# A GELU-gate kernel: 8-row tiles with two DMA queues, and 16-row blocks with one

## The chip, the core and the metric

The kernel runs on one core of a Trainium2 chip. The time is the device time of one execution in microseconds (us). Of the kernel before there are nine runs. Besides, one execution was recorded by the hardware profiler; all rows of "the profile" are from that one execution, with times counted from the first instruction of its span. In it DVE is VectorE, ACT is ScalarE, SP is SyncE, POOL is GpSimd; TensorE has no work here. "SPq" and "ACTq" are the instruction streams of SP and ACT as far as they issue DMAs. L81 is line 81 of the kernel.

## What is computed

```
x: float32 [32, 512, 2048]
x1, x2 = x[..., :1024], x[..., 1024:]
out = 0.5 * x1 * (1 + erf(x1 / sqrt(2))) * x2      # float32 [32, 512, 1024]
```

The input is 134.2 MB, the output 67.1 MB. Each value is read once, each result written once.

## The kernel before

The 32 x 512 = 16384 rows are cut into 16 tiles. A tile holds 8 rows (`R`) for each of the 128 partitions: partition p of a tile has 8 rows that follow one another in memory, so a load brings 64 KB of contiguous bytes to each partition (8.39 MB a tile), and a store takes 32 KB from each (4.19 MB).

There are two input buffers and two output buffers, used by turns (`k = i % 2`). For each tile, two steps of 5 and 3 rows: ACT computes gelu of the first half of each row into the output buffer (L81), then DVE multiplies the output buffer by the second half, in place (L89). The first and last tile are cut into three steps of 2, 2 and 4 rows.

The order of the work is written out by hand, with semaphores:

- Loads are all issued by SP (`load`, L47). The first tile's load is cut into two of 4 rows; it and tile 1's load are issued before anything else. In the loop, the load of tile i + 2 is issued when the multiplies of tile i are done (L108, L109), as it overwrites the same input buffer.
- Stores are issued by ACT (`store`, L54; called in L101 and L106) after the tile's multiplies, so that ACT's stream waits for DVE there. The store of tile 14 and the two half stores of tile 15 are issued by SP.
- Gelu of tile i waits on `ready[k]` (L79), which counts the load of tile i into input buffer k and the store that empties output buffer k: both must have landed.

Hence two queues carry DMAs at the same time, SP's with 64 KB for each partition and ACT's with 32 KB. Both run on the same 16 DMA engines. The kernel ends when SP has seen the last stores land (L118).

Of the kernel before, what the change touches and what calls it, by code (L numbers as in the profile page):

```python
# [1 line left out]

# [4 lines left out]

GELU = mybir.ActivationFunctionType.Gelu


@with_exitstack
def kernel(
    ctx: ExitStack,
    tc: tile.TileContext,
    x: bass.AP,
    out: bass.AP,
):
    nc = tc.nc
    P = nc.NUM_PARTITIONS

    x_flat = x.flatten_outer_dims()
    out_flat = out.flatten_outer_dims()
    n_rows, dim = x_flat.shape
    half = dim // 2

    R = 8
    x_t = x_flat.rearrange("(n p r) d -> n p r d", p=P, r=R)
    o_t = out_flat.rearrange("(n p r) d -> n p r d", p=P, r=R)
    n_tiles = x_t.shape[0]
    x_bufs = [nc.alloc_sbuf_tensor(f"x{k}_tile", [P, R, dim], x.dtype) for k in range(2)]  # L30
    o_bufs = [nc.alloc_sbuf_tensor(f"o{k}_tile", [P, R, half], out.dtype) for k in range(2)]

    first = [nc.alloc_semaphore(f"first{j}") for j in range(2)]
    ready = [nc.alloc_semaphore(f"ready{k}") for k in range(2)]
    gelu_done = nc.alloc_semaphore("gelu_done")
    mul_done = nc.alloc_semaphore("mul_done")
    tail_stored = nc.alloc_semaphore("tail_stored")
    n = {sem.name: 0 for sem in [*first, *ready, gelu_done, mul_done, tail_stored]}  # L40

    def counted(ins, sem, by):
        ins.then_inc(sem, by)
        n[sem.name] += by

    def load(i, rows, sem):
        ins = nc.sync.dma_start(out=x_bufs[i % 2][:, rows, :], in_=x_t[i][:, rows, :])  # L47
        counted(ins, sem, 16)
        return ins

    def store(queue, i, rows, sem):
        queue.wait_ge(mul_done, n[mul_done.name])
        counted(
            queue.dma_start(out=o_t[i][:, rows, :], in_=o_bufs[i % 2][:, rows, :]), sem, 16  # L54
        )

    for ins in (  # L60
        load(0, slice(0, 4), first[0]),
        load(0, slice(4, 8), first[1]),
        load(1, slice(0, 8), ready[1]),
    ):
        tc.no_tile_sem_insts.add(ins.ins.name)
    tc.close()
    tc.compile()  # L67

    for i in range(n_tiles):
        k = i % 2  # L70
        last = i == n_tiles - 1
        pieces = i == 0 or last
        steps = ((0, 2), (2, 4), (4, 8)) if pieces else ((0, 5), (5, 8))
        for lo, hi in steps:
            rows = slice(lo, hi)
            if i == 0 and lo % 4 == 0:
                nc.scalar.wait_ge(first[lo // 4], 16)
            elif lo == 0:
                nc.scalar.wait_ge(ready[k], n[ready[k].name])  # L79
            counted(  # L80
                nc.scalar.activation(  # L81
                    out=o_bufs[k][:, rows, :], in_=x_bufs[k][:, rows, :half], func=GELU
                ),
                gelu_done,
                1,
            )
            nc.vector.wait_ge(gelu_done, n[gelu_done.name])
            counted(
                nc.vector.tensor_mul(  # L89
                    out=o_bufs[k][:, rows, :],  # L90
                    in0=o_bufs[k][:, rows, :],
                    in1=x_bufs[k][:, rows, half:],
                ),
                mul_done,
                1,
            )
            if pieces and hi % 4 == 0:
                if last:
                    store(nc.sync, i, slice(hi - 4, hi), tail_stored)
                else:  # L100
                    store(nc.scalar, i, slice(hi - 4, hi), ready[k])  # L101
        if not pieces:
            if i == n_tiles - 2:
                store(nc.sync, i, slice(0, R), tail_stored)
            else:
                store(nc.scalar, i, slice(0, R), ready[k])  # L106
        if i + 2 < n_tiles:
            nc.sync.wait_ge(mul_done, n[mul_done.name])  # L108
            load(i + 2, slice(0, R), ready[k])  # L109


    nc.scalar.drain()  # L112
    for sem in (*first, *ready):
        nc.scalar.sem_clear(sem)
    nc.vector.drain()
    nc.vector.sem_clear(gelu_done)
    nc.sync.sem_clear(mul_done)
    nc.sync.wait_ge(tail_stored, n[tail_stored.name]).then_inc(  # L118
        tail_stored, -n[tail_stored.name]
    )  # L120


# [1 line left out]
_INS = ['x']  # L124
_OUTS = [((32, 512, 1024), 'float32')]


# [23 lines left out]
```

## Time and profile before

| What | Value |
|---|---|
| Median of nine runs | 469.21 us (469.13 to 469.47) |
| Profiled execution | 469.15 us |
| Its span, first to last instruction | 467.8 us |
| VectorE busy | 140.5 us, 34 multiplies |
| ScalarE busy | 115.5 us, 34 gelus and a table load |
| Gelu of 5 rows, of 3 rows | 4.47 us, 2.75 us |
| Multiply of 5 rows, of 3 rows | 5.49 us, 3.35 us |
| Read from HBM, written to it | 134.22 MB, 67.11 MB: 430 GB/s over the span |
| SP's DMA queue (q1) | 142.61 MB, 70.6% of the 16 engines' span |
| ACT's DMA queue (q10) | 58.72 MB, 29.1% |
| Store of a tile by ACT, issue to landing | 44.7 us (median of 13) |
| Load of a tile by SP, issue to landing | 44.3 us (median of 15) |
| ACT's gelu waited for a store to land | 301.7 us in 14 waits |
| ACT's gelu waited for a load | 35.6 us in 3 waits |

How to read it: a share of a queue is the time that its packets took, as a share of the time of 16 DMA engines over the span. "Issue to landing" runs from the instruction that starts a DMA until its last byte is reported. A wait is put down to what came last: gelu waits for a load and a store at once, and the profile names the later one.

### The profile page before, as it was taken

The page shows a single profiled execution, that of the slowest core. Times are in us where ns is not written, and L with a number is a line of the kernel's source. Part 1 is how long each engine was busy: PE and PEld are TensorE (multiplying, and loading weights), DVE is VectorE, ACT ScalarE, POOL GpSimd, SP SyncE. Part 2 cuts the span into 40 slices and gives each one's busy share as a digit, 9 for nine tenths or more (in the row PEclk, how much of TensorE's full clock was granted, in tenths as well). Part 3 has the DMA queues.
Part 4 walks back from the last instruction along what each step waited for, and adds up shares of the span by engine and source line. Part 5 has one row for each costly group of instructions (what it writes and reads, how often), then busy time and mean ns, then how long its engine had stood idle before and what let it go on. Part 6 is the DMA issues. An engine that isn't in the chain of part 4 may idle for free.

```text
span 467.8 us, 152 instructions
## 1 busy us (share of the span) xinstructions
DVE 140.5 (30%) x34; ACT 115.5 (25%) x35; POOL 0.2 (0%) x4
## 2 busy tenths in 40 slices
DVE  0330515207052060511606116060150702507043
ACT  1320606042060410604106050050500506014060
POOL 0000000000000000000000000000000000000000
DMA  8999999999999999999999999999999999999988
GB/s 359 448 448 448 415 389 496 403 403 448 448 448 403 434 417 493 403 403 448 482 415 403 445 406 493 403 403 448 488 409 403 448 420 476 403 420 431 493 381 382
DMA packets 5041, 201.34 MB, mean 430 GB/s; under 512 B 560, under 2 KB 560, under 8 KB 560
## 3 DMA queue, kind: packets, MB, share of 16 engines
q1 hardware_dynamic: 2880, 142.61, 70.6%
q10 hardware_dynamic: 2160, 58.72, 29.1%
q14 instruction: 1, 0.01, 0.0%
HBM read 134.22 MB, written 67.11 MB: 430 GB/s over the span
## 4 chain that ended last, share of the span: by engine, by line
DMA 76%; DVE 14%; ACT 8%; ACTq 0%; SPq 0%; issue 0%
DMA out_dram<-o_tile 66%; DVE o_tile L89 14%; DMA x_tile<-in_x_dram 10%; ACT o_tile L81 8%; ACTq L112 0%; SPq L47 0%
## 5 line engine op out<-in xcount | busy, mean ns | idle before, releaser
L89 DVE TENSOR_TENSOR o_tile<-o_tile,x_tile 128x5120 f32<-128x5120 f32 (+3 forms) x34 | 140.5, 4171 | 319.7 <-ACT o_tile L81 319.7
L81 ACT ACTIVATE o_tile<-x_tile 128x5120 f32<-128x5120 f32 (+3 forms) x34 | 114.3, 3407 | 337.4 <-DMA out_dram<-o_tile 301.7
L81 ACT ACT_TABLE_LOAD x1 | 1.3, 1283 | 2.8 <-PEq L67 2.8
L135 POOL MEMSET const-bfloat16-1.0<- 128x1 bf16 x1 | 0.1, 102 | 0.0
L135 POOL MEMSET const-uint8-127<- 128x1 uint8 x1 | 0.1, 102 | 0.0
L135 POOL MEMSET const-float32-1.0<- 128x1 f32 x1 | 0.1, 99 | 0.0
L135 POOL MEMSET const-float32-0.0<- 128x1 f32 x1 | 0.1, 98 | 0.2 <-issue 0.2
## 6 DMA issues: line engine op xcount, KB each, us to landing
out_dram<-o_tile ACTq DMA_DIRECT2D x13, 4096.0 KB, 44.7
x_tile<-in_x_dram SPq DMA_DIRECT2D x2, 4096.0 KB, 16.7
out_dram<-o_tile ACTq DMA_DIRECT2D x2, 2048.0 KB, 34.4
out_dram<-o_tile SPq DMA_DIRECT2D x1, 4096.0 KB, 25.2
out_dram<-o_tile SPq DMA_DIRECT2D x2, 2048.0 KB, 7.8
x_tile<-in_x_dram SPq DMA_DIRECT2D x15, 44.3
```

The lines of the kernel that those rows point to most:

```text
L81: nc.scalar.activation(out=o_bufs[k][:, rows, :], in_=x_bufs[k][:, rows, :half], func=GELU),
L89: nc.vector.tensor_mul(out=o_bufs[k][:, rows, :], in0=o_bufs[k][:, rows, :], in1=x_bufs[k][:, rows, half:],),
L135: nc = _bacc.Bacc("TRN2", target_bir_lowering=False, num_devices=1)
```

## The change

Two tiles become one block of 16 rows a partition. The block has two loads, A (its first 8 rows of each partition) and B (the other 8), each 64 KB a partition into its own input buffer, and one store of 64 KB a partition out of a single output buffer of 16 rows. All DMAs are issued by SP, in the order load A, store, load B; ACT issues none. The output buffers hold as many bytes as before.

- `load(b, h)`: half h of block b. The rows of neighbouring partitions now lie 128 KB apart in the input (64 KB before), and 64 KB apart in the output (32 KB before).
- Load A of block b + 1 is issued when A's multiplies of block b are done; the store of block b when B's are done, and load B of block b + 1 right after it.
- Gelu of half A waits on `ready[0]`: its load and the store of the block before. Gelu of half B waits on `ready[1]`: its load alone.
- The first block's loads are not cut (two whole loads are issued ahead instead of two halves and a whole one), and its steps are 5 and 3 rows. The last block's first half is stored by itself (32 KB a partition), its second half in steps of 2, 2 and 4 rows with two stores of 16 KB a partition.
- The multiplies and gelus are otherwise the same: 34 of each before and, with the first block's steps, 33 of each after. There are 26 DMAs instead of 35.

```diff
-    x_t = x_flat.rearrange("(n p r) d -> n p r d", p=P, r=R)
-    o_t = out_flat.rearrange("(n p r) d -> n p r d", p=P, r=R)
+    x_t = x_flat.rearrange("(n p h r) d -> n h p r d", p=P, h=2, r=R)
+    o_t = out_flat.rearrange("(n p r) d -> n p r d", p=P, r=2 * R)
...
-    o_bufs = [nc.alloc_sbuf_tensor(f"o{k}_tile", [P, R, half], out.dtype) for k in range(2)]
+    o_buf = nc.alloc_sbuf_tensor("o_tile", [P, 2 * R, half], out.dtype)
...
+    def load(b, h):
+        return counted(nc.sync.dma_start(out=x_bufs[h][:, :, :], in_=x_t[b, h]), ready[h], 16)
+
+    def store(b, rows, sem):
+        nc.sync.wait_ge(mul_done, n[mul_done.name])
+        counted(nc.sync.dma_start(out=o_t[b][:, rows, :], in_=o_buf[:, rows, :]), sem, 16)
...
-    for ins in (
-        load(0, slice(0, 4), first[0]),
-        load(0, slice(4, 8), first[1]),
-        load(1, slice(0, 8), ready[1]),
-    ):
-        tc.no_tile_sem_insts.add(ins.ins.name)
+    for h in range(2):
+        tc.no_tile_sem_insts.add(load(0, h).ins.name)
...
+    for b in range(n_blocks):
+        last = b == n_blocks - 1
+        for h in range(2):
+            nc.scalar.wait_ge(ready[h], n[ready[h].name])
+            for lo, hi in ((0, 2), (2, 4), (4, 8)) if last and h else ((0, 5), (5, 8)):
+                xr, orow = slice(lo, hi), slice(h * R + lo, h * R + hi)
...
+                if last and h and hi % 4 == 0:
+                    store(b, slice(R + hi - 4, R + hi), tail_stored)
+            if last and not h:
+                store(b, slice(0, R), tail_stored)
+            elif not last:
+                if h:
+                    store(b, slice(0, 2 * R), ready[0])
+                nc.sync.wait_ge(mul_done, n[mul_done.name])
+                load(b + 1, h)
```

More of the change, by code (lines that the diff above doesn't have):

```diff
@@ L26 @@
     R = 8
-    x_t = x_flat.rearrange("(n p r) d -> n p r d", p=P, r=R)
-    o_t = out_flat.rearrange("(n p r) d -> n p r d", p=P, r=R)
-    n_tiles = x_t.shape[0]
+    x_t = x_flat.rearrange("(n p h r) d -> n h p r d", p=P, h=2, r=R)
+    o_t = out_flat.rearrange("(n p r) d -> n p r d", p=P, r=2 * R)
+    n_blocks = x_t.shape[0]
     x_bufs = [nc.alloc_sbuf_tensor(f"x{k}_tile", [P, R, dim], x.dtype) for k in range(2)]
-    o_bufs = [nc.alloc_sbuf_tensor(f"o{k}_tile", [P, R, half], out.dtype) for k in range(2)]
-    first = [nc.alloc_semaphore(f"first{j}") for j in range(2)]
+    o_buf = nc.alloc_sbuf_tensor("o_tile", [P, 2 * R, half], out.dtype)
     ready = [nc.alloc_semaphore(f"ready{k}") for k in range(2)]
@@ L39 @@
     tail_stored = nc.alloc_semaphore("tail_stored")
-    n = {sem.name: 0 for sem in [*first, *ready, gelu_done, mul_done, tail_stored]}
+    n = {sem.name: 0 for sem in [*ready, gelu_done, mul_done, tail_stored]}
     def counted(ins, sem, by):
@@ L44, in counted @@
         n[sem.name] += by
-    def load(i, rows, sem):
-        ins = nc.sync.dma_start(out=x_bufs[i % 2][:, rows, :], in_=x_t[i][:, rows, :])
-        counted(ins, sem, 16)
-        return ins
[L51 to L55, printed above, removed]
-    for ins in (
-        load(0, slice(0, 4), first[0]),
-        load(0, slice(4, 8), first[1]),
-        load(1, slice(0, 8), ready[1]),
-    ):
-        tc.no_tile_sem_insts.add(ins.ins.name)
+        return ins
@@ L66 @@
+    def load(b, h):
[5 more added lines that the diff above has]
+        tc.no_tile_sem_insts.add(load(0, h).ins.name)
     tc.close()
     tc.compile()
[L69 to L109, printed above, removed]
@@ new lines @@
+    for b in range(n_blocks):
[4 more added lines that the diff above has]
+                xr, orow = slice(lo, hi), slice(h * R + lo, h * R + hi)
+                counted(
+                    nc.scalar.activation(
+                        out=o_buf[:, orow, :], in_=x_bufs[h][:, xr, :half], func=GELU
+                    ),
+                    gelu_done,
+                    1,
+                )
+                nc.vector.wait_ge(gelu_done, n[gelu_done.name])
+                counted(
+                    nc.vector.tensor_mul(
+                        out=o_buf[:, orow, :],
+                        in0=o_buf[:, orow, :],
+                        in1=x_bufs[h][:, xr, half:],
+                    ),
+                    mul_done,
+                    1,
+                )
+                if last and h and hi % 4 == 0:
[7 more added lines that the diff above has]
+                load(b + 1, h)
@@ L112 @@
     nc.scalar.drain()
-    for sem in (*first, *ready):
+    for sem in ready:
         nc.scalar.sem_clear(sem)
```

## The prediction, written before the changed kernel was run

> **What bounds the kernel now.** I read the page's busy lines first, then its slices, then the chain, the windows and the timeline.
>
> ```profile
> span 467.8 us, 152 instructions
> DVE 140.5 (30%) x34; ACT 115.5 (25%) x35; POOL 0.2 (0%) x4
> ...
> DMA  8999999999999999999999999999999999999988
> ...
> DMA 76%; DVE 14%; ACT 8%; ACTq 0%; SPq 0%; issue 0%
> ```
>
> No compute engine is busy for a third of the span; the DMA row is full except at its two ends. The chain names DVE and ACT for 22%, but that is only how one transfer is followed back through the buffer that it filled. Three stretches, asked for by window, decide between "the DMA engines are the limit" and "a loop of waits is the limit":
>
> ```profile
> 0.00:1.70 1.70, 0.00 (x0) 0.00 (x0) 0.20 (x4) 1.00 0.00 0
> 1.70:467.40 465.70, 140.49 (x34) 115.54 (x35) 0.00 (x0) 1.00 1.00 432
> 467.40:467.80 0.40, 0.00 (x0) 0.00 (x0) 0.00 (x0) 1.00 0.00 0
> ```
>
> The last two columns are the busy share of the 16 DMA engines and GB/s. Nothing moves for 1.7 us, then all engines are busy for 465.7 us, then 0.4 us pass until the last landing is seen. So the DMA engines' own time is the limit, not waits. Any kernel that moves these 201.3 MB at this rate can only gain at the ends or in the price of a packet.
>
> The steady period, from the timeline:
>
> ```profile
> 100.51 7.12 ACT L81 ACTIVATE o_tile<-x_tile 128x5120 f32<-128x5120 f32 x2 [21.88 <-DMA out_dram<-o_tile]
> 105.02 8.76 DVE L89 TENSOR_TENSOR o_tile<-o_tile,x_tile 128x5120 f32<-128x5120 f32 x2 [20.24 <-ACT o_tile L81]
> 113.81 0.36 ACTq L54 DMA_DIRECT2D out_dram<-o_tile  x1
> 129.51 7.12 ACT L81 ACTIVATE o_tile<-x_tile 128x5120 f32<-128x5120 f32 x2 [21.88 <-DMA out_dram<-o_tile]
> ```
>
> A tile (8.39 MB in, 4.19 MB out) takes 129.51 - 100.51 = 29.00 us, which is 434 GB/s, or 9.667 us for each 4.19 MB. From the first gelu of a tile to the end of its second multiply it is 113.80 - 100.51 = 13.3 us; call this the compute of a half block.
>
> The trace's packet records (one record for each piece that one DMA engine moves; here one partition's row of a DMA) give the price of a piece. From start to start on one engine: 64 KB 2.414 us, 32 KB 1.2095 us, 16 KB 0.607 us, and 0.0055 us more where one DMA ends and the next of the same queue begins. Eight pieces of 64 KB and eight of 32 KB make 28.99 us, which is the period: the engines run without gaps, and loads and stores cost the same per byte.
>
> **The change part by part.**
>
> *Same bytes, other pieces.* Before, for one DMA engine: loads 15 x 8 x 2.414 + 2 x 8 x 1.2095 = 309.03; stores 14 x 8 x 1.2095 + 4 x 8 x 0.607 = 154.89; together 463.92 us. After: 16 loads x 8 x 2.414 = 308.99; seven stores of 64 KB a partition 7 x 8 x 2.414 = 135.18; the half block 8 x 1.2095 = 9.68; two quarters 2 x 8 x 0.607 = 9.71; together 463.56. That is -0.36 us. DMAs go from 35 to 26: 9 x 0.0055 = -0.05. Sum **-0.4 us**. A 64 KB store piece is not in the trace; I price it as a 64 KB load piece, since at 32 KB both have a 1213 ns record. At two 32 KB pieces it would be 2.419, and this term -0.1.
>
> *The second queue goes.* Before, when the first store (ACT's queue) came beside the third load, the 64 KB records there were longer than 2418 ns, and again a little later: 0.39 us for a mean engine, all before 80 us. After, there is one queue and the first store comes at about 60 us behind work of its own queue. This can vanish (-0.39) or come back whole (0). I take half: **-0.2 us**.
>
> *One queue in order: does it run dry?* SP now issues everything: load A waits for A's multiplies, and behind it in SP's order stand the store and load B, which wait for B's multiplies. Follow one handover. When the store of block b lands, gelu of A(b+1) may start, since there is one output buffer. Its data landed 19.3 us earlier, as load A stands ahead of the store. It needs 13.3 us, then SP issues A(b+2). Meanwhile load B(b+1) runs for 2 x 9.667 = 19.3 us. The other handover is alike: B(b+1) lands, 13.3 us of compute, then the store and load B(b+2) are issued, while load A(b+2) runs for 19.3 us. A landing is seen 0.4 us after the last packet (467.4 to 467.8 above), and an issue needs 1.0 us to its first packet (0.73 to 1.7). So 13.3 + 0.4 + 1.0 = 14.7 us stand under a cover of 19.3 us: **slack 4.6 us**, cost nothing. If compute and latencies came to 19.3 + d, each of some 14 handovers would cost d.
>
> Does ACT or DVE slow down when the traffic beside it is all loads or all stores? The four 128x2048 multiplies ran two beside loads only (from 14.7 us) and two beside stores only (from 450.5 us); the pairs took 4.49 and 4.50 us. No.
>
> *The start.* Compute starts at about 22.5 us instead of 12.80, since the first load is whole. Loads A and B fill the queue until 1.7 + 0.6 (the first packets' excess) + 38.6 = 40.9 us; A's compute ends at 22.5 + 13.3 = 35.8, so the next issue again has 4 us of slack. Cost nothing; the old early store only filled a queue that was full.
>
> *The end.* The last loads land, then the half-block store (9.68 us, issued long before) covers the compute: the first quarter is ready 0.4 + 6.5 us after the last load (448.53 to 454.99 now), needed at 9.68; the second after 0.4 + 11.7 (to 460.22), needed at 14.5. No gap; the last DMA is 2 MB as before, so the end is unchanged. Before has this very sequence: load 15, store 14 and the last two stores, all on SP's queue:
>
> ```profile
> 432.80 27.76 SPq L54 DMA_DIRECT2D out_dram<-o_tile  x3
> 448.53 7.22 ACT L81 ACTIVATE o_tile<-x_tile 128x2048 f32<-128x2048 f32 x3 [21.89 <-DMA out_dram<-o_tile]
> ...
> 455.78 4.42 DVE L89 TENSOR_TENSOR o_tile<-o_tile,x_tile 128x4096 f32<-128x4096 f32 x1 [0.81 <-ACT o_tile L81]
> ```
>
> From 448.51 to 467.8 it stored 8.39 MB in 19.3 us, the steady rate. So pure stores on one queue, and load-then-store on one queue, are shown at full speed; so are pure loads (first two landings, 12.80 and 22.51: 9.71 us).
>
> *Store, then load, on one queue* happens seven times and is not in this trace. Nearest row: load to load, load to store and store to store, 0.0055 us each. Far row: the first packets of a cold engine, which were 0.6 us longer than the following ones. Below nothing there is nothing: no engine idles that a turn could fill. I take **0** (the queue has work behind it, as in the near rows); the far end is 7 x 0.6 = +4.2 us.
>
> *A rule against it.* The row pitch in HBM doubles: 128 KB between the partitions' rows of a load (64 KB before), 64 KB for a store (32 KB before). At the old pitches every steady packet took 2418 or 1213 ns. The trace shows no other pitch. The Trainium skill, "DMA: Bandwidth & Descriptors", section "Latency and other measured facts", says that copies between HBM tensors lose rate when the rows lie large powers of two apart: 207 GB/s at 512 KiB against 214 when padded, 164 at 2 MiB. As an estimate from that page, if its 512 KiB loss (3.3%) struck all loads, the time would be some 10 us more, about 478.7; its list starts above our pitch, so I count it as nothing.
>
> **Sum.** The profiled execution took 469.15 us (span 467.8 and 1.35 around it; the median of the runs is 469.21, 0.06 more). 469.15 - 0.4 - 0.2 = **468.55 us**.
>
> **Rivals.**
> 1. *Faster: the losses around the packets go too.* 465.7 us of traffic hold 463.9 + 0.2 us of pieces; some 1.5 us are the first packets' excess (0.6), the mixing (0.39) and the stagger of the 16 engines. A single orderly queue might lose less. Floor: 1.7 + 463.56 + 0.14 + 0.4 + 1.35 = 467.2. For it: the losses sit where queues start. Against: the 0.6 belongs to the cold start, which stays. With the mixing and most of the 0.6 gone: 467.8.
> 2. *Slower: the turn from store to load.* If the engine drained its store before it read again, every turn would cost up to 0.6 us: 468.55 + 4.2 = 472.8; at 0.35, 471.0. It decides from (470.15 - 468.55)/7 = 0.23 us a turn. Against: before, each engine goes from a store piece to a load piece eight times a tile, and the period equals the sum of pieces.
> 3. *The order does not hold or the queue does not take DMAs ahead*, so that each of 26 DMAs pays 1.0 + 0.4 us: 468.55 + 36 = 505. Against: store 14 was issued at 432.80 behind load 15 and ran after it without a gap.
>
> **Chances.** A measurement of this kernel can tell about 0.2% (0.94 us) from no change: faster means under 468.27, slower over 470.15. The forecast lies 0.3 us from the first bound, so the faster case takes a good share: forecast and what lies about it 0.60, rival 1 0.25, rival 2 0.12, rival 3 and the pitch 0.03. The range goes from the floor, 467.2, to the far end of the turns, 472.8; the forecast's own range, from the ends of its two terms, is 468.3 to 469.1.
>
> **What would show it.** Right: DMA share 1.00 from 1.7 us to 0.4 us before the end; blocks 58.0 us apart; gelu of A waiting for the store's landing, some 2 x 19.3 - 7.1 = 31.5 us, and gelu of B for load B's, 19.3 - 7.1 = 12.2 us; the SP queue's waits all for DVE. Wrong: a DMA share under 1 after each store (rival 2); records of 64 KB above 2418 ns through the steady part (pitch); handovers where an issue comes less than 1 us before the load in flight ends (slack); compute rows longer than 4.47 and 5.49 us.

## The result, and the profile after

The changed kernel takes 471.99 us (median of 9 runs, 471.40 to 473.45) against 469.29 us before (29 runs, 469.13 to 469.50): slower, ratio 1.0062, 95% interval 1.0054 to 1.0071. The prediction was 468.55 us, within 0.2% of no change. The time lies inside the range, but on the other side of the one that was held likely.

The profiled execution took 473.54 us, one of the longer ones. Its page, the lines that answer to those shown of before:

```profile
span 472.2 us, 139 instructions
...
DVE 140.3 (30%) x33; ACT 115.3 (24%) x34; POOL 0.2 (0%) x4
...
DMA  8999989999999999999999999999999999999988
...
q1 hardware_dynamic: 3744, 201.33, 99.1%
...
DMA 75%; DVE 14%; ACT 8%; SPq 1%; ACTq 0%; issue 0%
```

At first sight nothing has changed: the compute is the same, the DMA row is full, one queue now carries everything. The windows say where to look. Each goes from the gelu of one half block to the gelu of the next, that is, from landing to landing; the last two columns are the DMA engines' busy share and GB/s:

```profile
22.84:42.17 19.33, 8.76 (x2) 7.12 (x3) 0.00 (x0) 1.00 1.00 434
42.17:81.98 39.81, 8.76 (x2) 7.12 (x3) 0.00 (x0) 1.00 1.00 421
81.98:101.41 19.43, 8.76 (x2) 7.12 (x2) 0.00 (x0) 1.00 1.00 432
101.41:140.73 39.32, 8.76 (x2) 7.12 (x2) 0.00 (x0) 1.00 0.99 427
140.73:160.02 19.29, 8.76 (x2) 7.12 (x2) 0.00 (x0) 1.00 1.00 435
160.02:199.54 39.52, 8.76 (x2) 7.12 (x2) 0.00 (x0) 1.00 1.00 431
```

A window of 19.3 us holds one DMA, from a store's landing to load B's. These run at 432 to 435 GB/s, as before. A window of 39 us holds two, load A and then the store. At the steady rate it would be 38.7 us; the seven are 39.81, 39.32, 39.52, 39.34, 38.84, 39.11 and 38.68, together 3.7 us over. The last window of one DMA, load B of the last block, is 19.99, another 0.6 us over; behind that load the half-block store stands. So nearly all of the 4.4 us by which this execution is longer than the profiled one of before is lost in windows that hold a turn from load to store, while the busy share stays at 0.99 to 1.02 in those of the block stores. The reader is to see that this share cannot show the loss: a packet that takes longer counts as busy for longer. Nor do the GB/s of a window always: one of the long windows shows more than the steady rate, as engines that are ahead already move a part of the next DMA in it.

```profile
218.85:258.19 39.34, 8.76 (x2) 7.12 (x3) 0.00 (x0) 1.00 1.02 440
```

The length from landing to landing shows the loss, and so do the packets.

The packet records say which packet. I followed each of the 16 engines through its records. Nearly all are at 2418 ns. The exceptions are the first packet of all (0.78 us longer on average), and the last packet of load A, the one just ahead of the store on the same queue; together they hold 2.6 of the 3.15 us that a mean engine takes longer than its pieces' usual lengths. In the table, stores 1 to 7 are the block stores, 8 is the half-block store behind the last load B:

| Extra time of the last load packet ahead of store | 1 | 2 | 3 | 4 | 5 | 6 | 7 | 8 |
|---|---|---|---|---|---|---|---|---|
| after, mean of 16 engines, us | 1.03 | 0.21 | 0.31 | 0.15 | 0.01 | 0.09 | 0.05 | 0.12 |
| after, worst engine, us | 1.50 | 0.63 | 0.90 | 0.40 | 0.13 | 0.47 | 0.59 | 0.69 |

The mean falls quickly, the worst does not, and it need not be the same engine each time. A landing counts when the last of 16 engines is done. So the engines drift apart: before, they end their traffic within 0.42 us of each other (466.95 to 467.37), after within 1.64 us (470.20 to 471.84). They had been farther apart: they end the last load between 448.43 and 452.43 us, 13 of the 16 by 449.35. The first quarter store can be issued only when the slowest has landed and the compute is done, and near 459.5 us only 3 of 16 engines are moving data; the others stand still for up to 1.6 us. The windows from the last load's landing to the end of the span, after and then before:

```profile
452.74:472.20 19.46, 8.92 (x3) 7.21 (x3) 0.00 (x0) 1.00 0.79 338
448.53:467.80 19.27, 8.92 (x3) 7.22 (x3) 0.00 (x0) 1.00 0.95 409
```

The end itself is only 0.2 us longer, since the slowest engine, which ends last, does not stand still.

### The profile page after: what moved, and what is told of

It is laid out like the page before. It is cut to its first block, busy times and chain, and to the rows that moved or that the text cites. A ratio compares the mean times of both kernels' runs of the same rounds, so it can differ in the third digit from the quotient of the medians.

```text
span 472.2 us, 139 instructions
## 1 busy us (share of the span) xinstructions
DVE 140.3 (30%) x33; ACT 115.3 (24%) x34; POOL 0.2 (0%) x4
## 4 chain that ended last, share of the span: by engine, by line
DMA 75%; DVE 14%; ACT 8%; SPq 1%; ACTq 0%; issue 0%
DMA x_tile<-in_x_dram 75%; DVE o_tile L78 14%; ACT o_tile L70 8%; SPq L53 1%; ACTq L97 0%; SPq L49 0%
```

## The experiments

Theory 1: a store behind a load on the same queue stretches the load's last packets. Theory 2: the wider row pitch, the bigger store pieces or the single output buffer cost the time. Theory 3: issuing a big store disturbs what moves just then. Theory 4: the store is issued too late for the engine to look ahead.

**e4, loads in the place of the block stores** (the changed kernel, otherwise the same waits and order; `f_t` is half of a block of the input, and only the last block is written out).

```diff
...
-                    store(b, slice(0, 2 * R), ready[0])
+                    nc.sync.wait_ge(mul_done, n[mul_done.name])
+                    counted(nc.sync.dma_start(out=o_buf[:, :, :], in_=f_t[b, 0]), ready[0], 16)
```

> The changed kernel with its seven block stores replaced by loads of the same 64 KB a partition from x into the output buffer, after the same waits; only the last block is written out. One turn from load to store is left. Theory 1: 468.2 to 469.0, no long records until the last stores. If any DMA at this place of the queue, or the order with its late issues, costs the time: 471 to 473. Theory 3 with the issue of any DMA: 471 to 473.

Measured: 469.23 us, ratio 0.9999 (0.9989 to 1.0008). The windows of its trace, cut as above:

```profile
22.62:41.97 19.35, 8.76 (x2) 7.12 (x3) 0.00 (x0) 1.00 1.00 434
41.97:80.67 38.70, 8.76 (x2) 7.12 (x2) 0.00 (x0) 1.00 1.00 434
80.67:100.02 19.35, 8.76 (x2) 7.12 (x2) 0.00 (x0) 1.00 1.00 434
100.02:138.73 38.71, 8.76 (x2) 7.12 (x2) 0.00 (x0) 1.00 1.00 433
```

The two-DMA windows are 38.70 and 38.71 us, and the worst extra ahead of the replaced stores is 0.07 us. Order, waits, late issues and the 128 KB pitch of the loads cost nothing; the block stores do. Of theory 2 only the pitch and the pieces of the stores are left.

One turn from load to store remains in e4, the half-block store behind the last load, on the same queue and after 445 us of nothing but loads. It is free: the last packets of that load are at most 0.01 us longer. So a store behind a load on one queue does not always cost, and neither does a first store after a long run of loads.

**e2, the kernel before with all stores on SP's queue** (8-row tiles, two output buffers, a row pitch of 64 KB for loads and 32 KB for stores, nothing else changed).

```diff
-                    store(nc.scalar, i, slice(hi - 4, hi), ready[k])
+                    store(nc.sync, i, slice(hi - 4, hi), ready[k])
...
-                store(nc.scalar, i, slice(0, R), ready[k])
+                store(nc.sync, i, slice(0, R), ready[k])
```

> The kernel before with one edit: all its stores go on SP's queue (8-row tiles, two output buffers, 64 KB and 128 KB pitch unchanged from before). There are 15 turns from load to store in place of 8. Theory 1: slower than the changed kernel, since the turns double: 473 to 477. If each turn's stretch depends on how long the engines have moved one direction only, then less, 471 to 473. Theory 2 (pitch, pieces, single buffer): 469.3, as none of these is changed from before.

Measured: 474.77 us, ratio 1.0113 (1.0098 to 1.0128). Two of its tiles, which took 29.00 us before:

```profile
43.34:73.17 29.83, 8.76 (x2) 7.12 (x3) 0.00 (x0) 1.00 1.01 434
73.17:102.69 29.52, 8.76 (x2) 7.12 (x2) 0.00 (x0) 1.00 1.00 432
```

The later tiles take between 28.98 and 30.05 us. So the loss needs neither the pitch, nor the 64 KB store pieces, nor the single buffer: nothing of theory 2 is needed for it. It comes with one queue for both, and in these two kernels more turns cost more: 5.4 us with 15, 2.7 us with the changed kernel's 8.

**e3, no multiplies** (the output is gelu of the first half alone; stores issued 6 us earlier).

```diff
-        nc.sync.wait_ge(mul_done, n[mul_done.name])
+        nc.sync.wait_ge(gelu_done, n[gelu_done.name])
...
-                nc.vector.wait_ge(gelu_done, n[gelu_done.name])
-                counted(
-                    nc.vector.tensor_mul(
...
```

> The changed kernel without its multiplies (the output is gelu of the first half alone); SP waits for the gelus. Half a block's compute falls from 13.3 to 7.2 us, so every store is issued some 10.7 us ahead of its turn in place of 4.6. Theory 1: nothing changes, 471 to 473.5, and the long records stay the last ones of the load ahead of a store. Theory 3 (the issue disturbs): the long records move 6 us forward, to the load's packets that run just after the issue; time the same. Theory 4 (the store's descriptors come too late for the engine to look ahead): the long records go, 468.5 to 469.

Measured: 473.32 us, ratio 1.0080 (1.0065 to 1.0095). The extras stand at the same packets, the last ones ahead of a store: 0.93 us on average at the first, then 0.37, 0.43, 0.18. The windows are as long as the changed kernel's:

```profile
22.63:41.95 19.32, 7.12 (x2) 0.00 (x0) 1.00 1.00 434
41.95:81.93 39.98, 7.12 (x3) 0.00 (x0) 1.00 0.99 420
```

Theories 3 and 4 fall: neither the moment of the issue nor how far ahead it comes matters.

**e8, block 0's store alone** (blocks 1 to 6 as in e4).

```diff
...
+                    if b == 0:
+                        store(b, slice(0, 2 * R), ready[0])
+                    else:
+                        nc.sync.wait_ge(mul_done, n[mul_done.name])
+                        counted(nc.sync.dma_start(out=o_buf[:, :, :], in_=f_t[b, 0]), ready[0], 16)
```

> The kernel with loads in the place of block stores, but block 0's store put back; blocks 1 to 6 are not written out. It has the first turn and the last one of the changed kernel's eight. If the first turn carries the loss: 1.0 to 1.5 us above the kernel with no block store (469.23), 470.2 to 470.7. If the loss lies in the sum over the turns: 0.3 to 0.5 above, 469.6.

Measured: 470.21 us, ratio 1.0019 (1.0011 to 1.0028), 0.98 us above e4. The first such window, and the next:

```profile
41.94:81.89 39.95, 8.76 (x2) 7.12 (x3) 0.00 (x0) 1.00 0.99 420
101.10:139.78 38.68, 8.76 (x2) 7.12 (x2) 0.00 (x0) 1.00 1.00 434
```

That is the price of the first turn; the last turn of e8, its half-block store, is free again (no stretched packet). The other six stores of the changed kernel cost 471.99 - 470.21 = 1.78 us together, 0.3 us each.

**e5 and e6, one side of the turn at a time.** e5 copies from HBM to HBM in the place of the store (only the writing side turns), e6 from SBUF to SBUF (only the reading side). The marks behind # name the run.

```diff
...
-                    store(b, slice(0, 2 * R), ready[0])
+                    nc.sync.wait_ge(mul_done, n[mul_done.name])
+                    counted(nc.sync.dma_start(out=o_t[b], in_=f_t[b, 0]), ready[0], 16)                        # e5
+                    counted(nc.sync.dma_start(out=o_buf[:, R:, :], in_=o_buf[:, :R, :]), ready[0], 16)  # e6
```

> The changed kernel with its seven block stores replaced by copies of the same size from x straight to the output in HBM, after the same waits (so the output of those blocks is a part of x). The copy turns only the writing side of a DMA engine (SBUF to HBM), its reading side stays on HBM. What is read is not the total time, as the rate of such a copy is not in any trace yet, but the last load packet ahead of each copy. If the writing side's turn costs: those packets are stretched as in the changed kernel, about 1 us at the first, 0.1 to 0.6 later. If the reading side's turn costs: all at 2418 ns.

> The changed kernel with its seven block stores replaced by copies inside SBUF, from the output buffer's first 8 rows to its last 8 (4.19 MB each, half the bytes; those blocks are not written out). This turns only the reading side (HBM to SBUF), the writing side stays on SBUF. At the steady rate the time would be 469.2 - 7 x 9.667 = 401.5 us. If the reading side's turn costs, 402.5 to 405 and the last load packet ahead of each copy is stretched; if the writing side's, 401 to 402 and it stays at 2418 ns.

Measured, one execution each: e6 402.45 us against 401.5 at the steady rate. Three of its windows, each a load and a copy:

```profile
41.87:71.93 30.06, 8.76 (x2) 7.13 (x3) 0.00 (x0) 1.00 1.00 419
91.27:120.33 29.06, 8.76 (x2) 7.12 (x2) 0.00 (x0) 1.00 1.00 433
139.69:168.75 29.06, 8.76 (x2) 7.12 (x3) 0.00 (x0) 1.00 1.00 433
```

The first is 1.0 us long, all later ones run at the full rate, and only the packet ahead of the first copy is stretched (0.83 to 1.30 us). So the first 1 us needs no write to HBM. The later, smaller losses are missing without such writes; but the copies are half as long as the stores and it is one execution, so that they need the writes is suggested, not shown. e5 (510.32 us) shows no stretched load packet ahead of its copies, but the copies' own packets take 3.1 us on average in place of 2.4; with such copies nothing can be said of the later turns.

**e12, a small store first** (4 KB a partition behind the first two loads).

```diff
...
+    counted(nc.vector.memset(warm[:, :, :], 0.0), filled, 1)
+    nc.sync.wait_ge(filled, 1)
+    counted(nc.sync.dma_start(out=o_t[n_blocks - 1][:, 0:1, :], in_=warm[:, :, :]), ahead, 16)
...
```

> The changed kernel with a small store of zeros (4 KB a partition, a row that the last block overwrites) issued behind the first loads A and B, 20 us ahead of the first block store. If the 1 us is a price of the first read of SBUF after the start: it moves to the last packet of load B (about 38 us), and the last load packet ahead of block 0's store falls below 0.4 us; time as the changed kernel, 471.5 to 473. If it belongs to each first long store: it stays ahead of block 0's store, and the small one adds its own, 472.5 to 474.

Measured: 475.22 us, ratio 1.0126 (1.0111 to 1.0141), above what was expected. The packets say what was asked: load B's last packets, ahead of the small store, take 3.3 us (0.88 more), and those ahead of block 0's store 2418 ns exactly. So here the 1 us is paid once, by the store that comes first. The small store's own packets are 1.3 us for each engine; the other 1.9 us above the changed kernel are not explained.

**e7 and e11, half of the engines late.** A load of 8 partitions (32 KB each) ahead of everything (e7), or between the first loads A and B (e11), meant to make the engines turn in two groups.

```diff
...
+    tc.no_tile_sem_insts.add(
+        counted(nc.sync.dma_start(out=o_buf[0:8, 0:R, :], in_=j_t), ahead, 16).ins.name
+    )
...
```

> The changed kernel with one small load ahead of everything (8 partitions, 32 KB each, into the still empty output buffer), which occupies 8 of the 16 DMA engines for 1.2 us, so that two groups of engines come to each turn 1.2 us apart. If the stretch comes from 16 engines turning at the same moment: the first turn's stretch falls from 1.0 us to 0.5 or less, and the time is 469.2 + 1.2 = 470.4 at most for the late group, 470 to 471. If each engine pays by itself: first stretch about 1 us as before, time 472.5 to 474.

> The changed kernel with the small load for 8 engines (1.2 us) put between the first load A and the first load B instead of ahead of everything, so that the start is undisturbed. If the first turn's stretch of 1 us comes from 16 engines turning together: it falls to 0.5 or less and the time is 471 to 472.5 (1.2 us more work for half of the engines, 1 us less stretch). If it is a price of the first turn for each engine: 1 us stays, 473 to 474.

Measured: 475.25 us (ratio 1.0123, 1.0107 to 1.0138) and 476.54 us (1.0163, 1.0144 to 1.0181). Both failed as tests. The load was to hold up 8 engines for 1.2 us; instead it stretched packets on all 16, by 3.3 to 3.5 us in all on each in e11. In both, block 0's turn then shows no stretch, but whether that is the stagger or the price being paid earlier, as in e12, these runs can't tell.

**e9 and e10, more turns.** The kernel of e2 with each load and store cut into quarters; by turns (e9, 54 turns from load to store; not the 57 of the expectation), or four stores and then four loads (e10, 15 turns).

```diff
...
+            q = [slice(lo, lo + 2) for lo in range(0, R, 2)]
+            for rows in q:
+                if not pieces:
+                    store(nc.sync, i, rows, ready[k])
+                load(i + 2, rows, ready[k])                       # e10: a loop of its own
```

> The one-queue kernel with 8-row tiles (474.8 us), its loads and stores cut into quarters of 2 rows (16 KB and 8 KB a partition) and put on the queue by turns: quarter store, quarter load, and so on. Some 57 turns from load to store instead of 15. Compared with the next kernel, which has the same pieces with all four stores ahead of all four loads. If every turn costs about 0.25 us whatever the rhythm: 10 us above the next kernel. If turns at short intervals cost nothing (as in the kernel before, where each engine turns every 2.4 us): below the next one, by up to the 5 us that its turns cost.

> The same quarters with four stores, then four loads: 15 turns as in the one-queue kernel with 8-row tiles. Smaller pieces cost a little more each (16 KB 0.607 us against 2.414 for 64 KB is 0.6% more), so 474.8 + 3 to 5 = 478 to 480 with the turns' cost as it was.

Measured: 475.84 us (1.0139, 1.0124 to 1.0154) and 477.04 us (1.0164, 1.0148 to 1.0179), e10 a little under what was expected. The same pieces with 3.6 times the turns are not slower, but 1.2 us faster; the packets between 45 and 460 us hold 0.9 us of extra for a mean engine in e9, 1.6 in e10. A turn has no fixed price: turns every few us cost less each than turns after longer runs of one kind. Both kernels are slower than e2 (474.77 us), so the cut into quarters cost more than the finer alternation gave back.

**e1, the stores on ACT's queue, all else as changed.**

```diff
...
-                    store(b, slice(0, 2 * R), ready[0])
+                    store(nc.scalar, b, slice(0, 2 * R), ready[0])
```

> The seven block stores are issued by ACT instead of SP; blocks, 64 KB pieces, the single output buffer and all waits stay. Theory 1 (a store behind a load on the same queue stretches the load's last packets, 8 times): with two queues the stretch goes, 468.3 to 469.3 us, and records of 64 KB longer than 2.5 us only before 80 us. Theory 2 (the 128 KB row pitch, the 64 KB store pieces or the single output buffer cost the time): still 471 to 473. Theory 3 (the issue of a big store disturbs whatever moves in the few us after it): still 471 to 473, long records within 5 us of ACT's issues.

Measured: 529.99 us, ratio 1.1285 (1.1259 to 1.1311); all three expectations missed. The store now shares the engines with load B, and both land late and together. Two windows, from the store's landing on:

```profile
99.50:113.00 13.50, 9.03 (x3) 13.50 (x4) 0.00 (x0) 1.00 0.00 0
113.00:164.90 51.90, 8.40 (x2) 0.63 (x2) 0.00 (x0) 1.00 1.01 424
```

For 13.5 us nothing moves: with one output buffer, gelu of the next A waits for the store, and no load can be issued before it. The order on one queue is what lets one buffer do; the single buffer and the single queue belong together. The time says nothing of theory 1, but the packets do. The load packet ahead of each of the seven block stores is stretched on all 16 engines, by 1.00, 1.09, 1.18, 1.17, 1.12, 1.02 and 1.04 us on average, though the store is on the other queue, and from the second on that packet stands in the middle of a load. So the 1 us does not need a shared queue, and here it came back at every store, each time but the first after 13.5 us or so in which nothing moved.

**e13 and e14, the same long bursts on two queues and on one.** Loads are cut 7 + 1 rows and stores 14 + 2, so that the second queue can be started when the first part has landed, without overlapping the bursts; e14 is the same cut on SP's queue alone.

```diff
...
+                    nc.scalar.wait_ge(part[0], n[part[0].name])        # e13
+                    queue = nc.scalar                                  # e14: nc.sync
+                    queue.wait_ge(mul_done, n[mul_done.name])
+                    for rows, sem in ((slice(0, 14), most_stored), (slice(14, 16), ready[0])):
+                        counted(queue.dma_start(out=o_t[b][:, rows, :], in_=o_buf[:, rows, :]), sem, 16)
+                    nc.sync.wait_ge(most_stored, n[most_stored.name])  # e13
```

> The changed kernel's order with the block stores on ACT's queue, kept from overlapping: loads are cut 7 + 1 rows, block stores 14 + 2 rows; ACT issues the store when the first part of load A has landed, SP issues load B when the first part of the store has landed, so that the second parts (2.4 us each) cover the handover. If the shared queue costs the time: 469.3 to 470.6 (at most the first store's 1 us is left). If the long bursts cost it, whatever the queue: 471 to 473.5. If the handovers don't fit under 2.4 us (0.4 us landing + 1.0 us issue, and the engines' spread): the DMA share falls under 1 at each handover, over 474.

> The control: the same cut (7 + 1 rows, 14 + 2 rows) with all on SP's queue as in the changed kernel. 42 DMAs more and smaller pieces at the ends cost 0.3 to 0.5 us, so 472 to 473.5; both theories say the same.

Measured: e13 480.24 us (1.0229, 1.0199 to 1.0260), e14 473.43 us (1.0078, 1.0053 to 1.0102). In e13 the turn from load to store is free: no packet of load A is stretched ahead of the first store. The other turn costs instead:

```profile
81.12:101.31 20.19, 8.76 (x2) 7.12 (x2) 0.00 (x0) 1.00 0.97 415
101.31:140.09 38.78, 8.76 (x2) 7.12 (x3) 0.00 (x0) 1.00 1.02 433
140.09:160.43 20.34, 8.76 (x2) 7.12 (x3) 0.00 (x0) 1.00 0.96 412
```

The two-DMA windows are now 38.7 to 39.1 us, as good as free, but the windows from the store's landing to load B's, over all blocks, are 19.8 to 22.5 in place of 19.35. The first packets of load B are stretched, up to 1.2 us at the first turn and 1.7 us at the worst, where SP's queue starts again. Besides, engines stand still at the handovers between the queues, as in the third case of the expectation: 2.6 us on average between 30 and 450 us, against 0.2 us in e14. How much of the time goes to this, and how much to the stretch, the run does not tell apart. So this second queue is no cure: the loss at one turn goes and a greater one comes at the other. None of these versions beats the kernel before.

## Why the prediction was wrong

- **The bound and the slack were right up to the last block.** The DMA engines have work from 1.7 us on. No handover came late: e3 issued the stores 6 us earlier and gained nothing, and e4, with all the waits kept, ran at the rate of before. "No gap" at the end was wrong: the engines that were ahead stood still for up to 1.6 us near 460 us, as the quarter stores had to wait for the slowest one's load.
- **The pitch was right as nothing**, for the loads: e4's run at the full rate with rows 128 KB apart. e2 loses without any wider pitch.
- **The gains of 0.6 us were not seen.** The nearest thing to the changed kernel without its turns, e4, took 469.23 us against 469.34 of before in the same series, which is within its interval. The 0.4 us of fewer and larger pieces is too small to be told from the start's variations; it is not refuted either.
- **The step that failed** is "so pure stores on one queue, and load-then-store on one queue, are shown at full speed", and with it the near row of 0.0055 us for load to store. The row was load 15 and store 14, both on SP's queue. But in the packet records of before, load 15's last packet (443.9 us) and store 14's first (447.5 us) have a packet of ACT's store between them (446.3 us), and these engines had changed between loads and stores every 2.4 us for 400 us. It was not the case of eight load packets in a row and then eight of a store. In the changed kernel the turn from load to store, put at 0.0055 us, costs 1.0 us the first time and 0.3 us each time after. Whether the packet between is why the row was free is not shown: e4's last turn has none and is free too. The row was also read a little too well: the stores from 448.51 us on had begun at 447.5, and that window of before shows 409 GB/s.
- **The rival had the right sign and the wrong turn.** Rival 2 put up to 0.6 us on each turn from store to load. Those windows were free (19.3 to 19.4 us; the last, 19.99, ends with the load ahead of the half-block store); the loss came at the turn from load to store, on the load's last packet. That the time lies inside the range is owed to a bound that was set for the other turn.
- **The check that I named would have misled.** I said that a DMA share under 1 would show rival 2. The share stayed at 0.99 to 1.02 after the block stores; the length from landing to landing and the packet records showed it.
- **Averages hid the worst.** I priced a mean engine. What counts at each landing is the last of 16. Over all records, the extra of the changed kernel's engines runs from 2.2 to over 5 us, mean 3.15, against a mean of 0.99 before.

One rule of the skill bears on the step that failed, and differs from the runs. The Trainium skill, "DMA: Bandwidth & Descriptors", section "Issuing engines are not separate DMA queues", says that issuing from several engines saves no more than the time to issue. Here the stores' move from ACT's queue to SP's, with nothing else changed, cost 5.4 us (e2) where issue takes 0.36 us beside 29 us of transfer; the measurement decides.

What stays open: why an engine holds the load packet ahead of a store, why the extra dwindles for most engines and goes on for a few, and why two queues in long bursts (e13) pay at the other turn. That it is the bursts rather than the queue itself is what e1, e9 and e13 point to; it is not shown by a run that differs in that alone, and e4's last turn, free after the longest run of loads, speaks against the length of the run as the whole reason. That store has no load behind it in the queue, and e13's first store, free as well, had none issued until it was nearly done. Whether the load behind a store matters was not tested; the changed kernel's eighth turn, with no load behind it, still cost 0.12 us on average.

## What to carry to other kernels

When the DMA engines are the bound, don't take it as free to move the stores to the loads' queue: here that alone cost 5.4 us (e2). Finer alternation on one queue is not a cure by itself: it gained 1.2 us on the same pieces, and cutting the pieces cost more. Price a store behind a load on the same queue as something new if the trace has it only with other traffic between. Look for a slowdown of the DMAs in the time between landings, or in packet lengths, not in the busy share. Ask of each "near row" what else was moving at that moment.

## What the runs showed of the hardware

- The packet ahead of the first block store was about 1 us longer on every engine (1.03 us on average in the changed kernel); a copy that only reads SBUF does the same (e6: 0.83 to 1.30 us, then none), and a small store ahead takes it over (e12: 0.88 us). It is no rule for every first store: those of e4 (0.01 us at most) and e13 stretched nothing. In e1 it came back at each of seven stores (1.00 to 1.18 us), with the stores on another queue than the loads.
- Moving the stores from ACT's queue to SP's, with the loads, cost 5.4 us in 469.34 (e2).
- A load of 8 partitions, 0.26 MB, stretched packets on all 16 engines by 3.3 us and more (e11).
- Copies from HBM to HBM ran below the rate of loads and stores: a window of one load and one copy took 43.98 us in e5, against 38.7 for two loads in e4.
- After 13.5 us without traffic (e1) the first packets took mostly 0.5 to 0.9 us longer, much like those at the start of the kernel (0.78 us on average in the changed kernel).
